# Half of x on a second queue, a first scale made earlier, and a ninth quad of seven products in a one-core hybrid layer

## The chip, the cores and the metric

One core of a Trainium2 chip. The time is device microseconds of one execution; 1537.02 us is the median of three runs of the kernel before (1536.7 to 1537.57). Names of engines: PE is TensorE's matmul, PEld its weight load, DVE is VectorE, ACT is ScalarE, POOL is GpSimd, SP is SyncE, which here issues most of the DMAs.

## The reference

Batch 1, 256 rows, width 2048, one layer, all in fp32:

```python
mod = silu(c) @ ada_w + ada_b            # shift1, scale1, gate1, shift2, scale2, gate2
h = rms_norm(x, norm1_g) * (1 + sc1) + sh1
u, lru_gate, q, k, v, mix_gates = split(h @ w_in + b_in)
y_lru = rg_lru(conv(u)) * gelu(lru_gate)
y_attn = sliding_window_attention(q, k, v, sinks)
g_l, g_a = split(sigmoid(mix_gates))
x = x + g1 * ((g_l * (y_lru @ w_lru_out) + g_a * (y_attn @ w_attn_out)) @ w_o)
h2 = rms_norm(x, norm2_g) * (1 + sc2) + sh2
gate, up = split(h2 @ w_ffn_in)          # hidden width 5632
x = x + g2 * ((silu(gate) * up) @ w_ffn_out)
return rms_norm(x, final_g)
```

## The kernel before

**Products.** Weights are read once, in blocks of 128 x 1024 fp32 (0.5 MB, `raw`). ACT makes a rounded copy of a block (`hi`, L330) and DVE the rest (`lo`, L342), and PE takes three fp32r products for one fp32 product: hi by hi, lo by hi, hi by lo (`mm3`, L382 to L384; L1391 in the last matrix). The work is a list of items, one block each. `step` (L352) goes through it: it first issues what later items need (loads 6 ahead, copies 4, low parts 3), then the item's `before` hooks, then the item's products, then `run_sides`, which puts side work on DVE and ACT (above all the modulation columns) as far as a small model of the engines' clocks (`clock`) finds room. `posts` are what follows an item's last product, one stage of each per step. Every engine works its instructions in order.

**Modulation.** `ada_w` is read transposed, in halves of 0.5 MB (`aw`); one pass of DVE (L532) multiplies a half by the broadcast silu(c) (`crow`) and adds it up to one column of `modc`. 190 passes are needed; the first column of the first scale comes from PE instead (`sum_first`, L213, on two blocks `ak`). A column pair (shift, scale) of kt has to be there before the rows kt of h can be made.

**Opening.** SP issues `vec`, four quarters of x transposed (`xT`, L143), the two `ak` blocks, and then `aw`, `wf` (weights of the first four slabs) and `raw` by turns. PE does warm passes on ones (`keep_warm`, L162; `N_WARM` is how many at three places), broadcasts silu(c) into `crow` (L182), and sums the first scale. ACT squares x quarter by quarter and DVE adds up (`squares`). The sum over partitions (`ssc`) goes to PE between the two halves of `sum_first`; then root, reciprocal, diagonal, a product that spreads the root over partitions (`rx_ps`), and the first `hx`. `First` multiplies k-tiles 0 and 1 in plain fp32 for four slabs (L663), 13.4 us of PE, while `hi`, `lo` and columns for the list are made. The list's first items have few k-tiles each, as `h` comes k-tile by k-tile (`cuts`).

**Second norm.** Items of `w_o` end the first part of the layer; after them `second_norm` follows. `hold_sides`, a hook of the last item but one of `w_o`, stops side work until then. `ada_to(3, 4)`, which makes sure that all columns of shift2 and scale2 are done, is called at the fourth slab of `w_o`.

**Seven products for eight.** From the hidden layer on, some quads (two k-tiles by two column blocks, on two row halves) are done by seven products instead of eight (`seven`, L427). Such a quad needs `wx` (sums of blocks, made by accumulating DMAs that POOL issues 16 and 11 items ahead), `wy` (two DVE additions, L458 and L459) and sums of the left side. A seven has four items, the products of one, two, two and two blocks. In the last matrix (`w_ffn_out`, two halves of 1024 columns, `w_f2a` and `w_f2d`) 18 pairs of k-tiles come in the order of `TURNS`; `SEVEN` says which are sevens. There the left sums are made by `f_parts` in the hidden layer, and split by `parts_high` and `parts_low` (`ah`, `al`, L1404 and L1409), hooks of the two items that stand three and two before a seven's first. After a half's last seven `combined` adds up its banks in five stages, on DVE. The second half ends with eight more items: four for one column block (`w_f2b`) and four, for the upper rows first, of the last block (`w_f2c`), then `last_rows` for the lower rows (`late`), and the final norm.

Of the kernel before, what the change touches and what calls it, by code (L numbers as in the profile page):

```python
# [9 lines left out]
F32 = mybir.dt.float32  # L10
F32R = mybir.dt.float32r
AF = mybir.ActivationFunctionType
# [4 lines left out]
P = 128  # L17
D = 2048
S = 256
# [26 lines left out]

N_K = 1

N_WARM = (6, 15, 5)

N_WARM_2 = (2, 5)

# [12 lines left out]
N_MADE, N_HOLD = 5, 4  # L65

N_SUM = (16, 11)
SEVEN = tuple(range(6, 36, 4))

SEVEN_1, SLAB_7 = (4, 6, 10, 12), 1  # L70

SLAB_G = 4
TURNS_1 = {1: "---7-77-"}

TURNS = "--7-7-7-7-7-7-7-7-"
EARLY = NH - 2 * N_HOLD

N_SPARE = 5
# [5 lines left out]
def hybrid_layer(  # L84
# [21 lines left out]
    def b4(name, dt=F32, shape=(4, S)):  # L106
        used["b4"] += 1
        return bp.tile([P, *shape], dt, tag="b4", name=name)
# [9 lines left out]
    def wtile(name):  # L118
        return ps.tile([P, 2, S], F32, tag="bank", name=name)
# [8 lines left out]
    def rows(t):  # L128
        return slice(t * P, (t + 1) * P)
# [6 lines left out]
    vec = const.tile([P, NV], F32, name="vec")  # L136
    nc.sync.dma_start(vec, vecs)

    def load_x(name):
        ts = []  # L140
        for q in range(4):
            t = b4(f"{name}{q}")
            nc.sync.dma_start(t, x_t[:, 4 * q:4 * q + 4, :])  # L143
            ts.append(t)
        return ts

    xT = load_x("xT")
    first = [b4(f"ak{i}", F32, (NK // 2, P)) for i in range(2)]
    for i in range(2):
        nc.sync.dma_start(first[i], ada_k[i])  # L150
    ones = const.tile([P, P], F32, name="ones")
    nc.vector.memset(ones, 1.0)
    eps_t = const.tile([P, 1], F32, name="eps_t")
# [4 lines left out]
    def keep_warm(n, of_w=False):  # L158

        warm = in_rows_of(wtile("warm")) if of_w else mtile("warm")  # L160
        for _ in range(n):
            nc.tensor.matmul(warm[:, 0:P], lhsT=ones, rhs=ones, start=True, stop=True)  # L162
        free(m=0 if of_w else 1)

    keep_warm(N_WARM[0])

    cact = const.tile([P, NK], F32, name="cact")
# [16 lines left out]

    def squares(q):

        for h in ((slice(0, 4),) if q < 3 else (slice(0, 2), slice(2, 4))):
            nc.scalar.activation(sqx[q][:, h, :], xT[q][:, h, :], AF.Square)
        a = sqx[q]
        for n in (2, 1):  # L190
            nc.vector.tensor_tensor(a[:, 0:n, :], a[:, 0:n, :], a[:, n:2 * n, :], op=ALU.add)
        if q in (1, 2):
            nc.vector.tensor_tensor(a[:, 0, :], a[:, 0, :], sqx[q - 1][:, 0, :], op=ALU.add)

    def c_rows(a, b):
        for i in range(a, b):
            nc.vector.tensor_copy(crow_of(i), c_ps[i])
            free(m=1)

    keep_warm(N_WARM[1])  # L200
    c_rows(0, 1)
    squares(0)
    c_rows(1, 3)
    squares(1)
    c_rows(3, 4)
    squares(2)
    squares(3)

    sc_ps = wtile("sc_ps")[:, 0, 0:P]

    def sum_first(a, b):
        for k in range(a, b):
            nc.tensor.matmul(  # L213
                sc_ps, lhsT=cact[:, k:k + 1].broadcast_to([P, P]), rhs=first[k // 8][:, k % 8, :],
                start=k == 0, stop=k == NK - 1,
            )
# [130 lines left out]
    def upto(what, fn, n):  # L347
        while at[what] < min(n, len(items)):
            fn(at[what])
            at[what] += 1  # L350
# [353 lines left out]
    def ada_to(*ms):  # L704
        while not {(m, kt) for m in ms for kt in range(NK)} <= cols_done:
            if not ada.advance():
                clock["pe"] += 1
                halves.fetch()
# [339 lines left out]
    def load_rows(s):  # L1048
        def before():
            xr.append(b4(f"xr{s}", F32, (2, 512)))  # L1050
            nc.sync.dma_start(xr[s], x_r[:, s * 512:(s + 1) * 512].rearrange("(t p) n -> p t n", p=P))
            if s == 3:
                ada_to(3, 4)
        return before

    def keep_rows(s):
# [29 lines left out]

    def hold_sides():

        clock["slack"] = -1e9
        return 0, 0  # L1090

    items[-2].before.append(hold_sides)

    def turn(p, of_w=False):

# [507 lines left out]
    fetch_to(6)  # L1603
    begin.load(1)

    sum_first(0, NK // 2)
    ssc = mtile("ssc")
    for t in range(2):
        for q in (2, 3):
            nc.tensor.matmul(  # L1610
                ssc[:, t:t + 1], lhsT=sqx[q][:, 0, rows(t)], rhs=ones[:, 0:1], start=q == 2, stop=q == 3,
                skip_group_check=True,
            )
    rc = sp.tile([P, 2], F32, tag="rc", name="rc")
    nc.scalar.activation(rc, ssc[:, 0:2], AF.Sqrt, bias=eps_t, scale=1.0 / D)
    free(m=1)
    sum_first(NK // 2, NK)

    def until(cols):
        while not cols <= cols_done:  # L1620
# [10 lines left out]
    keep_warm(N_WARM[2])  # L1631
    rx = sp.tile([P, S], F32, tag="rx", name="rx", bufs=1)
    nc.scalar.copy(rx, rx_ps)

    dst = modc[:, 1, 0:1]
    nc.vector.tensor_tensor_reduce(
        out=sqx[0][:, 1, 0:P], in0=sc_ps, in1=ident, op0=ALU.mult, op1=ALU.add, scale=1.0,
        scalar=vec[:, V_ADA + NK:V_ADA + NK + 1], accum_out=dst,
    )
    nc.vector.scalar_tensor_tensor(dst, dst, 1.0, vec[:, V_N1:V_N1 + 1], op0=ALU.add, op1=ALU.mult)  # L1640
    cols_done.add((1, 0))
    until({(0, 0)})
    x0 = xT[0][:, 0, :]
    nc.vector.scalar_tensor_tensor(x0, x0, dst, rx_ps, op0=ALU.mult, op1=ALU.mult)
# [16 lines left out]
    upto("hi", do_hi, 1)  # L1661
    upto("lo", do_lo, 1)
    hmod.advance(True)
    for n in range(2):
        begin.post(n)
    upto("hi", do_hi, 2)
    until({(0, 2), (1, 2)})
    fetch_to(14)
    begin.post(2)
    hmod.finish_to(lambda: 2 in h_done)  # L1670
    upto("lo", do_lo, 2)
    upto("hi", do_hi, 3)
    upto("lo", do_lo, 3)
    begin.post(3)
    clock.update(pe=T_START[0], dve=T_START[1], act=T_START[1])
    halves.spare = lambda: len(halves.got) - halves.own < N_SPARE
# [11 lines left out]
def _layout(i):  # L1688
# [10 lines left out]
    def pairs(w):  # L1699
# [13 lines left out]
    w2 = f("w_ffn_out")[0]  # L1713
    a_k = ada_w[:, D:D + P].reshape(2, NK // 2, P, P).transpose(0, 2, 1, 3)
    made = {
        "vecs": vecs, "x_t": f("x")[0].T.reshape(NK, P, S).transpose(1, 0, 2), "x_r": f("x")[0], "ada_k": a_k,
        "ada_t": a_t,
        "w_in": slabs(f("w_in")[0]), "bv_row": f("b_in")[0, 6656:7168], "bm_row": f("b_in")[0, 7168:], "lru_w": lru,
        "w_lru": slabs(f("w_lru_out")[0]), "w_att": slabs(f("w_attn_out")[0]), "w_o": slabs(f("w_o")[0]),
# [25 lines left out]
```

## Time and profile before

| what | us |
|---|---|
| median of three runs | 1537.02 (1536.7 to 1537.57) |
| profiled execution, its own time | 1538.73 |
| its span, first to last instruction | 1537.0 |
| PE busy | 1521.0 |
| DVE busy | 1365.3 |
| ACT busy | 880.7 |

The profile is one execution. Its page gives busy times, strips of 40 slices, the chain of work that ended last, and groups of instructions. Matmuls are pipelined and their ends are modelled, so a row's duration of a product (0.39 us) is longer than the distance to the next (0.228 us); the distances are what PE takes. A wait is put down to the one that came last. The granted clock is given as a share of 2.4 GHz; the other level is 0.50, 1.2 GHz.

### The profile page before, as it was taken

How to read it: one execution, taken by the hardware profiler on the slowest of the kernel's cores; microseconds unless marked ns; L12 is line 12 of the kernel's file. 1: busy time of each engine (PE TensorE's matmuls, PEld its weight loads, DVE VectorE, ACT ScalarE, POOL GpSimd, SP SyncE). 2: the span in 40 equal slices, each digit the busy share in tenths (PEclk: the TensorE clock that was granted, in tenths of full speed). 3: DMA queues.
4: the chain of work that ended last, by engine and by line, in shares of the span. 5: the costliest groups of instructions: out<-in, count | busy, mean ns of one | idle time of the engine just before them, and what ended most of it. 6: DMA issues, size and time to landing. Idle time of an engine off the chain costs nothing.

```text
span 1537.0 us, 20204 instructions
## 1 busy us (share of the span) xinstructions
PE 1521.0 (99%) x6851; PEld 1249.0 (81%) x6851; DVE 1365.3 (89%) x1835; ACT 880.7 (57%) x1142; POOL 163.5 (11%) x232
## 2 busy tenths in 40 slices
PE   8999999999999999999999999999999999999997
PEld 5788888888888787888887878888888888888886
DVE  7999999888898888988988899999999999888987
ACT  4654444886964446444444556656665556664664
POOL 0000000000000000000002231034212122321200
PEclk9999999999999999999999999999999999999999
DMA  9999988656786887999999999589898979989983
GB/s 368 383 345 362 345 315 301 207 181 217 241 286 226 291 308 283 364 325 341 377 373 347 312 338 273 167 254 332 274 273 248 269 243 298 288 257 297 275 266 124
DMA packets 138440, 444.58 MB, mean 289 GB/s; under 512 B 16064, under 2 KB 16224, under 8 KB 138336
## 3 DMA queue, kind: packets, MB, share of 16 engines
q1 hardware_dynamic: 113056, 384.02, 70.2%
q0 software_dynamic: 24992, 58.75, 16.1%
q8 instruction: 53, 0.87, 0.2%
q10 hardware_dynamic: 288, 0.52, 0.1%
q14 instruction: 51, 0.42, 0.1%
HBM read 439.02 MB, written 4.21 MB: 288 GB/s over the span
## 4 chain that ended last, share of the span: by engine, by line
PE 93%; DMA 3%; DVE 3%; ACT 0%; issue 0%; SPq 0%; DVEq 0%; ACTq 0%
PE pf L1391 10%; PE f L383 6%; PE f L382 6%; PE f L384 6%; PE wi L383 6%; PE wi L384 6%; PE wi L382 6%; PE wl L384 2%; PE wl L383 2%; PE wga L384 2%; PE wl L382 2%; PE wga L382 2%; PE wgl L383 2%; PE wga L383 2%; PE wgl L384 2%; PE wa L384 2%
## 5 line engine op out<-in xcount | busy, mean ns | idle before, releaser
L330 ACT CAST hi<-raw 128x1024 fp32r<-128x1024 f32 (+1 forms) x540 | 532.3, 996 | 419.1 <-PE wi L384 87.4
L342 DVE TENSOR_TENSOR lo<-raw,hi 128x1024 fp32r<-128x1024 f32 (+1 forms) x540 | 611.9, 1149 | 82.1 <-issue 37.7
L383 PE MATMUL wi<-lo,h 128*128 128x512 f32 x432 | 168.4, 390 | 3.3 <-DVE lo L342 3.3
L382 PE MATMUL wi<-hi,h 128*128 128x512 f32 x432 | 169.9, 393 | 0.0
L384 PE MATMUL wi<-hi,h 128*128 128x512 f32 x432 | 168.2, 389 | 0.0
L382 PE MATMUL f<-hi,h 128*128 128x512 f32 x406 | 158.8, 391 | 0.0
L383 PE MATMUL f<-lo,h 128*128 128x512 f32 x406 | 158.1, 389 | 0.0
L384 PE MATMUL f<-hi,h 128*128 128x512 f32 x406 | 158.0, 389 | 0.0
L532 DVE CUSTOM_DVE_ANT_0 aw<-aw,crow,vec 128x1024 f32<-128x1024 f32 x95 | 120.5, 1277 | 6.0 <-DMA aw<-in_ada_t_dram 6.0
L532 DVE CUSTOM_DVE_ANT_0 aw<-aw,crow,modc 128x1024 f32<-128x1024 f32 x95 | 121.1, 1277 | 1.6 <-DMA aw<-in_ada_t_dram 1.6
L330 ACT CAST hi<-wy 128x1024 fp32r<-128x1024 f32 x55 | 58.0, 1055 | 74.3 <-PE f L384 32.1
L383 PEld LDWEIGHTS wi<-lo,h 128*128 128x128 f32 x432 | 81.1, 188 | 20.9 <-DVE lo L342 4.3
L342 DVE TENSOR_TENSOR lo<-wx,hi 128x1024 fp32r<-128x1024 f32 x55 | 67.2, 1222 | 32.4 <-issue 28.5
L330 ACT CAST hi<-wx 128x1024 fp32r<-128x1024 f32 x55 | 58.0, 1055 | 64.8 <-PE pf L1391 24.0
L382 PEld LDWEIGHTS wi<-hi,h 128*128 128x128 f32 x432 | 81.1, 188 | 16.8 <-ACT acc L611 0.2
L384 PEld LDWEIGHTS wi<-hi,h 128*128 128x128 f32 x432 | 81.1, 188 | 16.7
L384 PEld LDWEIGHTS f<-hi,h 128*128 128x128 f32 x406 | 76.2, 188 | 15.8
L383 PEld LDWEIGHTS f<-lo,h 128*128 128x128 f32 x406 | 76.2, 188 | 15.7 <-DVE lo L342 0.3
L382 PEld LDWEIGHTS f<-hi,h 128*128 128x128 f32 x406 | 76.2, 188 | 15.6
L447 POOL DMA_DIRECT2D wx<-in_w_f_dram x78 | 69.8, 969 | 79.5 <-DMA wx<-in_w_f_dram 78.4
L443 POOL DMA_DIRECT2D wx<-in_w_f_dram x78 | 44.7, 627 | 287.6 <-DVE lo L342 95.2
L342 DVE TENSOR_TENSOR lo<-wy,hi 128x1024 fp32r<-128x1024 f32 x55 | 67.2, 1222 | 6.9 <-ACT hi L330 4.3
(347 smaller groups left out, 3094.1 us busy)
## 6 DMA issues: line engine op xcount, KB each, us to landing
aw<-in_ada_t_dram SPq DMA_DIRECT2D x190, 512.0 KB, 6.7
raw<-in_w_in_dram SPq DMA_DIRECT2D x164, 512.0 KB, 5.1
raw<-in_w_f_dram SPq DMA_DIRECT2D x137, 512.0 KB, 6.5
wx<-in_w_f_dram POOLq DMA_DIRECT2D x156, 256.0 KB, 7.9
raw<-in_w_f2a_dram SPq DMA_DIRECT2D x36, 512.0 KB, 6.4
raw<-in_w_lru_dram SPq DMA_DIRECT2D x32, 512.0 KB, 4.6
raw<-in_w_att_dram SPq DMA_DIRECT2D x32, 512.0 KB, 5.5
raw<-in_w_o_dram SPq DMA_DIRECT2D x32, 512.0 KB, 8.1
```

The lines of the kernel that those rows point to most:

```text
L330: nc.scalar.copy(hi[:, cs], live[i][0][:, cs])
L342: nc.vector.tensor_tensor(lo[:, cs], raw[:, cs], f32(hi[:, cs]), op=ALU.subtract)
L382: nc.tensor.matmul(ps, lhsT=lh, rhs=rh, start=start, stop=False, skip_group_check=True)
L383: nc.tensor.matmul(ps, lhsT=lh, rhs=rl, start=False, stop=False, skip_group_check=True)
L384: nc.tensor.matmul(ps, lhsT=ll, rhs=rh, start=False, stop=stop, skip_group_check=True)
L443: nc.gpsimd.dma_start(x[:, j * 512:(j + 1) * 512], block(0, 1))
L447: nc.gpsimd.dma_start(got["x"][:, j * 512:(j + 1) * 512], block(j, j), accum_op=ALU.add)
L532: nc.vector.tensor_tensor_reduce(out=r, in0=r, in1=crow[j], op0=ALU.mult, op1=ALU.add, scale=1.0, scalar=dst if j else vec[:, v:v + 1], ac ...
L1391: nc.tensor.matmul(bank(t, n), lhsT=l[:, rows(t)], rhs=w[:, c0:c0 + 512], start=kt == 0 and k == 0, stop=kt == (EARLY - 2 if (t, n) == (1, ...
```

## The change

Opening: x is laid out in four contiguous quarters. SP issues quarters 0 and 2, each before an `ak` block; ACT issues quarters 1 and 3, after a small Silu activation. The 15 warm passes of `N_WARM[1]` (30 records) are gone, the third number goes from 5 to 6. `c_rows` and `squares` are in another order, and the last quarter's squares are added in two halves that go to PE apart. All of `sum_first` and DVE's use of it come before the squares' sums (the diff leaves out the same DVE lines where they stood before, behind `rx`). In the steps before the list, low parts and modulation passes go by turns. At the end of `w_o`, `hold_sides` sits one item earlier and calls `ada_to(3, 4)`. In the last matrix k-tiles 2 and 3 become a seven too: nine of 18, strictly by turns with plain quads.

```diff
-N_WARM = (6, 15, 5)
+N_WARM = (6, 0, 6)
-SEVEN = tuple(range(6, 36, 4))
+SEVEN = tuple(range(2, 36, 4))
-TURNS = "--7-7-7-7-7-7-7-7-"
+TURNS = 9 * "-7"
-    xT = load_x("xT")
+    xT = [b4(f"xT{q}") for q in range(4)]
     first = [b4(f"ak{i}", F32, (NK // 2, P)) for i in range(2)]
-    for i in range(2):
-        nc.sync.dma_start(first[i], ada_k[i])
+    for t, from_ in ((xT[0], x_t[0]), (first[0], ada_k[0]), (xT[2], x_t[2]), (first[1], ada_k[1])):
+        nc.sync.dma_start(t, from_)
...
+    nc.scalar.activation(sp.tile([P, 1], F32, tag="st", name="silu"), eps_t, AF.Silu)
+    for q in (1, 3):
+        nc.scalar.dma_start(xT[q], x_t[q])
     keep_warm(N_WARM[0])
...
-        for h in ((slice(0, 4),) if q < 3 else (slice(0, 2), slice(2, 4))):
-            nc.scalar.activation(sqx[q][:, h, :], xT[q][:, h, :], AF.Square)
         a = sqx[q]
+        if q == 3:
+            for h in range(2):
+                nc.scalar.activation(a[:, 2 * h:2 * h + 2, :], xT[q][:, 2 * h:2 * h + 2, :], AF.Square)
+                nc.vector.tensor_tensor(a[:, 2 * h, :], a[:, 2 * h, :], a[:, 2 * h + 1, :], op=ALU.add)
+            return
+        nc.scalar.activation(a, xT[q], AF.Square)
...
-    keep_warm(N_WARM[1])
-    c_rows(0, 1)
+    sc_ps = wtile("sc_ps")[:, 0, 0:P]
+    c_rows(0, 2)
     squares(0)
-    c_rows(1, 3)
+    c_rows(2, 4)
     squares(1)
-    c_rows(3, 4)
     squares(2)
     squares(3)
...
-            if s == 3:
-                ada_to(3, 4)
...
     def hold_sides():
+        ada_to(3, 4)
         clock["slack"] = -1e9
         return 0, 0
-    items[-2].before.append(hold_sides)
+    items[-3].before.append(hold_sides)
...
-    sum_first(0, NK // 2)
+    sum_first(0, NK)
+    dst = modc[:, 1, 0:1]
+    nc.vector.tensor_tensor_reduce(
+        out=sqx[0][:, 1, 0:P], in0=sc_ps, in1=ident, op0=ALU.mult, op1=ALU.add, scale=1.0,
+        scalar=vec[:, V_ADA + NK:V_ADA + NK + 1], accum_out=dst,
+    )
+    nc.vector.scalar_tensor_tensor(dst, dst, 1.0, vec[:, V_N1:V_N1 + 1], op0=ALU.add, op1=ALU.mult)
+    cols_done.add((1, 0))
     ssc = mtile("ssc")
-    for t in range(2):
-        for q in (2, 3):
+    for i, x in enumerate((sqx[2][:, 0, :], sqx[3][:, 0, :], sqx[3][:, 2, :])):
+        for t in range(2):
...
-    sum_first(NK // 2, NK)
...
     hmod.advance(True)
-    for n in range(2):
-        begin.post(n)
+    begin.post(0)
     upto("hi", do_hi, 2)
+    ada.advance(True)
+    upto("lo", do_lo, 2)
+    begin.post(1)
+    ada.advance(True)
+    ada.advance(True)
+    upto("hi", do_hi, 3)
+    begin.post(2)
+    upto("lo", do_lo, 3)
     until({(0, 2), (1, 2)})
     fetch_to(14)
-    begin.post(2)
     hmod.finish_to(lambda: 2 in h_done)
-    upto("lo", do_lo, 2)
-    upto("hi", do_hi, 3)
-    upto("lo", do_lo, 3)
     begin.post(3)
...
-        "x_t": f("x")[0].T.reshape(NK, P, S).transpose(1, 0, 2)
+        "x_t": f("x")[0].T.reshape(4, 4, P, S).transpose(0, 2, 1, 3)
```

## Rows read from the trace of the kernel before

**Rows 1.** Page, parts 1 and 2: busy us (share) xinstructions; DMA strip, 40 slices

```profile
PE 1521.0 (99%) x6851; PEld 1249.0 (81%) x6851; DVE 1365.3 (89%) x1835; ACT 880.7 (57%) x1142; POOL 163.5 (11%) x232
...
DMA  9999988656786887999999999589898979989983
```

**Rows 2.** Who waited for whom, PE, whole run: us in total, times, longest

```profile
PE wi L383 <- DVE lo L342: 3.3, 2, 1.7
```

**Rows 3.** Chain that ended last, 0 to 62 us: start us, us, what

```profile
1.66 0.42 SPq L143
...
19.88 7.80 DMA raw<-in_w_in_dram
...
39.70 9.22 DMA raw<-in_w_in_dram
...
52.66 0.50 PE wi L383
```

**Rows 4.** Windows: length, busy us of PE, PEld, DVE, ACT, POOL, clock, DMA share, GB/s

```profile
4.00:5.00 1.00, 0.72 (x1) 0.50 (x2) 1.00 (x3) 0.93 (x2) 0.00 (x0) 1.00 0.82 238
```

**Rows 5.** Timeline of ACT in the opening: start us, us, instruction [idle before]

```profile
0.75 1.28 ACT L168 ACT_TABLE_LOAD   x1 [0.75 <-PEq L1733]
...
5.03 1.06 ACT L188 ACTIVATE sqx<-xT 128x1024 f32<-128x1024 f32 x1
8.20 1.06 ACT L188 ACTIVATE sqx<-xT 128x1024 f32<-128x1024 f32 x1 [2.12 <-DMA xT<-in_x_t_dram]
...
10.77 1.15 ACT L188 ACTIVATE sqx<-xT 128x512 f32<-128x512 f32 x2 [0.21 <-DMA xT<-in_x_t_dram]
```

**Rows 6.** Timeline of DVE, 14 to 20 us

```profile
14.75 1.28 DVE L532 CUSTOM_DVE_ANT_0 aw<-aw,crow,vec 128x1024 f32<-128x1024 f32 x1 [0.67 <-DMA aw<-in_ada_t_dram]
...
17.20 0.35 DVE L1636 CUSTOM_DVE_ANT_0 sqx<-sc_ps,ident,vec 128x128 f32<-128x128 f32 x1 [0.77 <-PE sc_ps L213]
...
19.39 0.35 DVE L1646 TENSOR_SCALAR hx<-xT,modc 128x256 f32<-128x256 f32 x1
```

**Rows 7.** Timeline of PE in the opening, warm passes and half of the first scale

```profile
1.06 2.93 PE L162 MATMUL warm<-ones 128*128 128x128 f32 x12 [1.06 <-DVE eps_t L154]
...
9.19 3.51 PE L162 MATMUL warm<-ones 128*128 128x128 f32 x30
...
15.13 2.03 PE L213 MATMUL sc_ps<-ak,cact 128*128 128x128 f32 x16
```

**Rows 8.** Chain, 1296 to 1345 us: plain quads of the last matrix

```profile
1314.86 5.44 PE pf L1391 x24
...
1325.06 5.44 PE pf L1391 x24
```

**Rows 9.** Timeline of DVE at the start of the last matrix

```profile
1301.87 2.95 DVE L342 TENSOR_TENSOR lo<-raw,hi 128x1024 fp32r<-128x1024 f32 x3
1304.75 1.08 DVE L1409 TENSOR_TENSOR al<-fs,ah 128x896 fp32r<-128x896 f32 x1
```

**Rows 10.** Timeline of DVE at the start of its second half

```profile
1411.91 0.69 DVE L1461 TENSOR_TENSOR y<-pf,g 128x512 f32<-128x512 f32 x1 [0.31 <-PE pf L1391]
...
1413.24 1.22 DVE L342 TENSOR_TENSOR lo<-raw,hi 128x1024 fp32r<-128x1024 f32 x1
...
1425.46 1.23 DVE L342 TENSOR_TENSOR lo<-wy,hi 128x1024 fp32r<-128x1024 f32 x1
```

**Rows 11.** DVE at the end: groups of 1500.4 to 1524.1 us, then its timeline

```profile
L342 DVE TENSOR_TENSOR lo<-raw,hi 128x1024 fp32r<-128x1024 f32 x8 | 9.7, 1217 | 0.0
...
1526.67 0.55 DVE L1461 TENSOR_TENSOR y<-late,g 128x384 f32<-128x384 f32 x1
...
1529.11 0.29 DVE L1461 TENSOR_TENSOR y<-late,g 128x128 f32<-128x128 f32 x1 [1.30 <-PE late L384]
```

**Rows 12.** Windows at the second norm, columns as in rows 4

```profile
826.00:829.00 3.00, 1.33 (x9) 0.94 (x8) 2.38 (x6) 2.41 (x7) 0.00 (x0) 1.00 1.09 298
...
830.00:833.00 3.00, 3.00 (x14) 2.81 (x13) 2.55 (x6) 1.62 (x5) 1.98 (x4) 0.50 1.04 406
```

More of the change, by code (lines that the diff above doesn't have):

```diff
@@ L137, in hybrid_layer @@
     nc.sync.dma_start(vec, vecs)
[L139 to L145, printed above, removed]
-    xT = load_x("xT")
+    xT = [b4(f"xT{q}") for q in range(4)]
     first = [b4(f"ak{i}", F32, (NK // 2, P)) for i in range(2)]
-    for i in range(2):
-        nc.sync.dma_start(first[i], ada_k[i])
+    for t, from_ in ((xT[0], x_t[0]), (first[0], ada_k[0]), (xT[2], x_t[2]), (first[1], ada_k[1])):
+        nc.sync.dma_start(t, from_)
     ones = const.tile([P, P], F32, name="ones")
@@ L198, in c_rows @@
             free(m=1)
-    keep_warm(N_WARM[1])
-    c_rows(0, 1)
+    sc_ps = wtile("sc_ps")[:, 0, 0:P]
+    c_rows(0, 2)
     squares(0)
-    c_rows(1, 3)
+    c_rows(2, 4)
     squares(1)
-    c_rows(3, 4)
     squares(2)
     squares(3)
-    sc_ps = wtile("sc_ps")[:, 0, 0:P]
     def sum_first(a, b):
@@ L1604, in hybrid_layer @@
     begin.load(1)
-    sum_first(0, NK // 2)
+    sum_first(0, NK)
[6 more added lines that the diff above has]
+    cols_done.add((1, 0))
     ssc = mtile("ssc")
-    for t in range(2):
-        for q in (2, 3):
+    for i, x in enumerate((sqx[2][:, 0, :], sqx[3][:, 0, :], sqx[3][:, 2, :])):
+        for t in range(2):
             nc.tensor.matmul(
-                ssc[:, t:t + 1], lhsT=sqx[q][:, 0, rows(t)], rhs=ones[:, 0:1], start=q == 2, stop=q == 3,
+                ssc[:, t:t + 1], lhsT=x[:, rows(t)], rhs=ones[:, 0:1], start=i + t == 0, stop=i == 2,
                 skip_group_check=True,
@@ L1633, in hybrid_layer @@
     nc.scalar.copy(rx, rx_ps)
[L1635 to L1641, printed above, removed]
     until({(0, 0)})
@@ L1715, in _layout @@
     made = {
-        "vecs": vecs, "x_t": f("x")[0].T.reshape(NK, P, S).transpose(1, 0, 2), "x_r": f("x")[0], "ada_k": a_k,
+        "vecs": vecs, "x_t": f("x")[0].T.reshape(4, 4, P, S).transpose(0, 2, 1, 3), "x_r": f("x")[0], "ada_k": a_k,
         "ada_t": a_t,
```

## The prediction

> **What bounds the kernel now.** I read part 1 and the strips of the page first, then who waited for whom on PE, then the chain, then the timelines of the three places the diff touches. PE is busy 99% of the span, so a change has to take products away or close one of PE's few gaps [rows 1]. Over the run PE waits 3.3 us, in two waits, for a low part in the input projection, and nothing else costs it as much [rows 2]. The strip of the DMA engines is full in its first slices [rows 1]: the opening lives on transfers. The chain shows it. A weight block issued at 19.88 needs 7.80 us to land, one issued at 39.70 needs 9.22 us, and the second of PE's waits ends at 52.66, 3.7 us after that block landed at 48.92 [rows 3]. So PE's state at 52.7 us is set by how many bytes have come, not by when PE began. From there to the two waits at the second norm PE has no wait over 0.2 us, so whatever the opening gains or loses by 52.7 is carried to the end.
>
> **Opening, transfers.** Four quarters of x (2.1 MB) and two blocks of the first scale (1.05 MB) come ahead of the modulation columns and weights. The same bytes come before and after; two of the quarters now go out on ACT's queue and interleave with SP's. Only an emptier stretch of the DMA engines can give time back. Between 4 and 5 us they moved 238 GB/s [rows 4]. ACT's square of the second quarter waited 2.12 us for it, until 8.20; the next two quarters were there by 10.77 [rows 5], 1.28 us each (0.52 MB, 408 GB/s). The second came 3.2 us after the first (5.0), so at most 1.9 us are to be had. From the other side, ACT issues its first quarter only behind a table load that ends at 2.03 and an added 0.2 us activation, 0.6 us later than SP issued it (1.66) [rows 3, 5]: 0.6 us can be lost. I take a gain of 0.5 us, nearer to no change, because the first quarter, in the same layout, showed no such lag, and the later blocks all run at the full rate: it looks like a matter of the first microseconds rather than of the layout or the queue. The Trainium skill (DMA: Bandwidth & Descriptors, "Issuing engines are not separate DMA queues") says that starting transfers from several engines saves only the issuing time, as all run on the same 16 engines. By that rule the gain is nothing and the sum 0.5 us longer; the issue of 0.42 us for a quarter that takes 1.28 us bears it out so far.
>
> **Opening, order.** The first scale's 32 passes now all run before the squares' sums, and DVE's work on them (0.35 and 0.16 us) stands ahead of its first modulation pass. Before, that pass ran at 14.75 and DVE then stood until 17.20 for the scale [rows 6]. That looks like 1.2 us. But the second scale block is still the last of the same 3.3 MB and lands near 13.3; its 16 passes take 2.03 us [rows 7], so DVE gets the scale at 15.3, and the pass that ran at 14.75 now waits behind it until 15.9. The two passes, the root's reciprocal and diagonal (0.5 us) and the two steps of `hx` then end at about 19.6 against 19.74 now [rows 6]: nothing won. Low parts by turns with passes closes the first wait (1.7 us at 36.8 to 38.3): the second item's low part no longer stands behind four passes. It is not banked: the fourth item's low part still comes after the same DVE work, at 42.4, and the eighth item waits for its block at 48.9 as before. PE's idle 1.7 us there is the cover that hides all of this. The 30 warm passes (3.51 us) taken out and one fp32 pass added (0.25 us) lie in PE's waiting.
>
> **Second norm.** `hold_sides` comes one item earlier; the columns it demands are done by 742 us, so `ada_to` does nothing in either place. One modulation pass (1.28 us) moves from before the norm to after it. The low part that gates the norm is bound by its own block's landing, so I take 0, between -0.3 and +0.5. Slab 0 of the hidden layer now makes a sum form of one pair: 0.3 us more on DVE, beside PE.
>
> **Ninth quad.** A plain quad is 24 products in 5.44 us, and plain and seven together recur every 10.20 us, so a seven takes 4.76 [rows 8]. One more in each half: 2 x 0.68 = 1.36 us less PE. In the steady alternation DVE has 1.4 us free in 10.2, and nothing changes there. The edges change, since a quad of plain products that stood as a cushion at the start and end of each half is gone.
> Start of the first half: DVE finishes the hidden layer's last gating at 1301.87 [rows 9]. Before, two plain quads (10.9 us) follow; now one, and DVE must do a half low part (0.6), `al` (1.0), `wy` (1.33) and a low part (1.22) by the seven's second item: 1306.0. PE reaches that product at 1303.6 + 0.8 (transposes) + 0.68 + 0.23 = 1305.3: 0.7 us of stall, 0 to 1.2.
> Start of the second half: four residual pairs of 1.33 us (1411.91 to 1413.24) interleave with the same list. From 1413.2: 0.6, 1.0, 1.33, 1.33, 1.13, 1.33, 1.13, 1.33, 1.22 end the `wy` low part at 1423.6; before it ended at 1426.7 [rows 10]. PE wants it at 1413.3 + 5.44 + 0.68 + 2 x 1.36 + 0.23 = 1422.4: 1.2 us, 0 to 1.6.
> The end: after the last product of sevens (1500.3) DVE works without a break until it takes the first late block at 1526.67, and the second at 1529.11, when PE has it; eight subtractions cost 9.7 us there [rows 11]. Now PE has one plain quad less to run after that product (5.44), DVE two subtractions less (2.3). DVE reaches the second late block at 26.4 - 2.3 + 1.1 = 25.2 us after it, or 24.9 if its small waits go too, and PE at 28.8 - 5.44 = 23.4. The last rows become DVE's: 1.5 us, 0 to 2.
>
> **Sum.** -0.5 (opening) + 0 (norm) - 1.36 + 0.7 + 1.2 + 1.5 = +1.5, which I round down to +1.4 because small DVE waits can close. The profiled execution took 1538.73 us (span 1537.0, 1.7 around it), so it would take 1540.1; the median of the runs lies 1.7 lower, and 1537.02 becomes **1538.4 us**. With the bounds of the terms it goes from about 1536 to 1541.
>
> **Rivals.** *DVE keeps up.* Its queue has three low parts in hand at each edge; if the orders mesh, no stall shows. For it: the page has hardly any such wait now. Against: the counts above. -1.36 - 0.5: 1535.2.
> *Both gains arrive.* The quarters come at the late rate (1.9 us) and the edges are covered: -3.3, 1533.7, faster. For it: the slow stretch is exactly the second quarter.
> *The clock falls in the opening,* the slower one. PE loses its 30 passes and stands idle from 9.4 until the first scale block is here. At the second norm, after a stretch with 1.33 us of products in 3, the granted clock went from 1.00 to 0.50 [rows 12], that is from 2.4 to 1.2 GHz. The first 12 warm passes took 2.93 us, the later 30 took 3.51 [rows 7], so at the low level 32 passes cost 4 us more, and the first products begin near 23.5 and run 3 us or more at half speed. The cover of 1.7 us is then used up and about 2 us remain: 1540.6. It decides if the first block lands after about 11 us, and not if it lands at 10, as I expect from its place behind two quarters. The Trainium skill (TensorE: Matmul & The Clock Gate, "Why this matters for your kernels") warns against idle gaps between bursts for this reason; that gap in this kernel is not yet in any row.
>
> **How the numbers follow.** Forecast (DVE takes the quads' gain back) 0.55, DVE keeps up 0.20, both gains 0.13, clock 0.12. 0.2% is 3.1 us, about what runs of this kernel can tell from no change: faster means under 1533.9, slower over 1540.1. Faster: the third case and a little of the second, 0.15. Slower: most of the clock's case and the top of the forecast's, 0.15. Same: 0.70. The range takes in the forecast with its bounds and both outer cases: 1533.5 to 1541.0.
>
> **What would show it.** Right: PE's wait near 38 us gone, the one near 50 us still there and ended by DVE behind a landed block; PE waits for DVE of about a microsecond soon after the first plain quad of each half; DVE idle-free to the last two late blocks, with PE done first. Wrong: first weight blocks landing over 1.5 us earlier than 27.7; no wait at the halves' starts; a clock of 0.50 between 10 and 25 us.

## The result, and the profile after

The changed kernel takes 1542.86 us (median of five runs, 1541.19 to 1544.38) beside 1536.7 for the kernel before (five runs, 1536.09 to 1537.57): 1.0038 times as long, 95% interval 1.0024 to 1.0051. It is slower; 1538.4 was forecast. The profiled execution of after took 1542.86 with a span of 1541.1.

PE has less work, as the change means it to, and DVE more. The page's part 1 answers [rows 1].

```profile
PE 1518.0 (99%) x6821; PEld 1244.1 (81%) x6821; DVE 1373.6 (89%) x1848; ACT 885.1 (57%) x1150; POOL 169.0 (11%) x240
```

PE's waits of the whole run answer [rows 2]: us in total, times, longest.

```profile
PE wi L381 <- DVE lo L340: 3.2, 2, 1.7
PE fr L381 <- DVE lo L340: 1.4, 1, 1.4
...
PE pu L380 <- DVE fl L989: 0.9, 1, 0.9
...
PE pq L381 <- DVE lo L340: 0.8, 1, 0.8
...
PE pf L381 <- DVE lo L340: 0.5, 1, 0.5
PE f L381 <- DVE lo L340: 0.4, 1, 0.4
```

The two waits of the opening are still there (`wi`, one now for the fourth item's low part, until 42.2, the other until 52.3). New are two in the hidden layer's second slab (`f`, `fr`, at 902 to 905 us) and three at the starts of the last matrix's halves (`pf`, `pu`, `pq`). Windows show the first pair's price: length, busy us of the engines, granted clock, DMA share, GB/s.

```profile
826.00:829.00 3.00, 2.16 (x17) 1.92 (x16) 1.50 (x6) 1.17 (x5) 0.00 (x0) 1.00 1.07 326
830.00:833.00 3.00, 3.00 (x17) 2.48 (x17) 2.81 (x8) 1.38 (x4) 0.61 (x2) 1.00 0.98 395
...
902.00:906.00 4.00, 2.22 (x8) 1.26 (x7) 4.00 (x6) 2.51 (x3) 1.98 (x3) 0.94 1.12 227
905.00:909.00 4.00, 3.52 (x9) 2.80 (x9) 3.96 (x6) 1.09 (x2) 1.06 (x2) 0.57 1.08 301
```

At the second norm the clock now stays at 1.00, where [rows 12] have 0.50. Behind the two waits at 902 to 905 it falls instead to 0.50, 1.2 GHz: nine products in four us where, at 0.228 us each, seventeen fit.

DVE's timeline at the starts of the two halves answers [rows 9] and [rows 10]; the last two lines are the end, as in [rows 11].

```profile
1302.18 0.69 DVE L340 TENSOR_TENSOR lo<-raw,hi 128x512 fp32r<-128x512 f32 x1
1302.78 1.08 DVE L1406 TENSOR_TENSOR al<-fs,ah 128x896 fp32r<-128x896 f32 x1
...
1305.12 1.22 DVE L340 TENSOR_TENSOR lo<-raw,hi 128x1024 fp32r<-128x1024 f32 x1
1306.25 1.22 DVE L340 TENSOR_TENSOR lo<-wx,hi 128x1024 fp32r<-128x1024 f32 x1
1307.39 1.22 DVE L340 TENSOR_TENSOR lo<-wy,hi 128x1024 fp32r<-128x1024 f32 x1
1308.52 1.28 DVE L989 TENSOR_TENSOR fl<-ft,fh 128x512 fp32r<-128x512 f32 x2
...
1413.45 0.69 DVE L1458 TENSOR_TENSOR y<-pf,g 128x512 f32<-128x512 f32 x1
...
1423.98 1.22 DVE L340 TENSOR_TENSOR lo<-wy,hi 128x1024 fp32r<-128x1024 f32 x1
...
1531.91 0.55 DVE L1458 TENSOR_TENSOR y<-late,g 128x384 f32<-128x384 f32 x1
...
1532.97 0.28 DVE L1458 TENSOR_TENSOR y<-late,g 128x128 f32<-128x128 f32 x1
```

The list at 1302 to 1308 is the one counted in the prediction, with `fl` behind it, which was not counted. At the end DVE takes both late blocks (`late`) without a pause between them, and PE's last product is over at 1531.4: the end waits for DVE, as forecast.

Distances between products give what each place costs. The stretch from the first product behind the second norm to `g_ps` (the next gate) took 178.8 us before and 181.2 after. The last matrix, from its first product to its last, took 230.9 and 232.9: 1.36 us less work, 1.85 us of waits at the first half's start and 1.44 at the second's. From PE's last product to the end of the span there are 7.9 and 9.6 us. These three lengths are followed through the experiments.

### The profile page after: what moved, and what is told of

It reads as the page before. It is cut to its first block, busy times and chain, and to the rows that moved or that the text cites. A ratio compares the mean times of both kernels' runs of the same rounds, so it can differ in the third digit from the quotient of the medians.

```text
span 1541.1 us, 20198 instructions
## 1 busy us (share of the span) xinstructions
PE 1518.0 (99%) x6821; PEld 1244.1 (81%) x6821; DVE 1373.6 (89%) x1848; ACT 885.1 (57%) x1150; POOL 169.0 (11%) x240
## 5 line engine op out<-in xcount | busy, mean ns | idle before, releaser
L1388 PE MATMUL pf<-hi,fc 128*128 128x512 f32 x288 | 79.9, 389 | 0.0
L445 POOL DMA_DIRECT2D wx<-in_w_f_dram x78 | 69.8, 979 | 83.8 <-DMA wx<-in_w_f_dram 83.1
```

The costliest lines, as they stand in the source:

```text
L445: nc.gpsimd.dma_start(got["x"][:, j * 512:(j + 1) * 512], block(j, j), accum_op=ALU.add)
L1388: nc.tensor.matmul(bank(t, n), lhsT=l[:, rows(t)], rhs=w[:, c0:c0 + 512], start=kt == 0 and k == 0, stop=kt == (EARLY - 2 if (t, n) == (1, ...
```

## Experiments

Times are medians; the ratio is to the kernel before on the same chip (medians of 1535.7 to 1536.7 by group), with its 95% interval. It is not simply the quotient of the two medians, and can differ from it by up to 0.001. The last three columns are the lengths just named, from the one profiled execution of each run.

| run | us | ratio | hidden | last matrix | end |
|---|---|---|---|---|---|
| before | 1536.7 | | 178.8 | 230.9 | 7.9 |
| after | 1542.86 | 1.0038 [1.0024, 1.0051] | 181.2 | 232.9 | 9.6 |
| hold_alone | 1538.54 | 1.0019 [1.0010, 1.0028] | 180.2 | 230.9 | 7.9 |
| quads_alone | 1540.54 | 1.0029 [1.0019, 1.0040] | 178.7 | 232.9 | 9.6 |
| opening_alone | 1536.93 | 0.9998 [0.9989, 1.0007] | 177.9 | 230.9 | 8.1 |
| quads_back | 1539.82 | 1.0021 [1.0012, 1.0030] | 182.8 | 230.9 | 8.1 |
| hold_back | 1540.71 | 1.0030 [1.0019, 1.0041] | 178.2 | 233.0 | 9.9 |
| pair_12 | 1543.40 | 1.0052 [1.0039, 1.0064] | 180.4 | 233.0 | 9.8 |
| no_load | 1539.74 | 1.0022 [1.0012, 1.0032] | 178.2 | 233.0 | 9.9 |
| no_pass | 1540.77 | 1.0029 [1.0019, 1.0039] | 179.9 | 233.0 | 9.6 |
| cushion | 1539.14 | 1.0020 [1.0009, 1.0031] | 178.7 | 234.2 | 8.2 |
| no_wy | 1538.40 | 1.0014 [1.0005, 1.0023] | 178.2 | 230.3 | 9.9 |
| fl_early | 1540.08 | 1.0024 [1.0014, 1.0034] | 180.3 | 232.6 | 9.9 |
| pool_wy | 1544.78 | 1.0059 [1.0047, 1.0072] | 179.7 | 239.0 | 10.1 |
| opening_warm | 1535.64 | 0.9995 [0.9986, 1.0004] | 178.8 | 230.9 | 8.1 |
| opening_sp | 1536.83 | 1.0003 [0.9993, 1.0013] | 179.9 | 230.9 | 8.1 |

### Which part costs

**quads_back** is the changed kernel with the sevens as they were:

```diff
-SEVEN = tuple(range(2, 36, 4))
+SEVEN = tuple(range(6, 36, 4))
-TURNS = 9 * "-7"
+TURNS = "--7-7-7-7-7-7-7-7-"
```

> The changed kernel with its eight sevens per half and their old order back; opening, second norm and hold_sides stay as changed. The two traces, laid side by side, give this ledger against the kernel before: opening -0.3, second norm -3.0 (1.7 of it a stretch at clock 0.50 that is gone), a stall with a stretch at clock 0.50 behind it at 902 to 909 us +3.2, starts of the halves +3.3, the products saved -1.4, the end +1.8. Theory S (slab 0's sum form, which only the ninth seven needs, makes DVE late at 902 us): stall and edges go, the norm's gain stays, 1533 to 1534.5. Theory P (the modulation pass moved behind the norm makes it late): the stall stays, 1536.5 to 1537.5, and PE waits over 1 us for a low part near 903 us. In both the halves' starts have no wait over 0.3 us.

The waits near 903 stay (`f` 1.8, `fr` 1.4 us), so slab 0's sum form, theory S, is out. The last matrix and its end are back to 230.9 and 8.1. But the time, 1539.82, is 2 to 3 us over what theory P gave. The ledger in that expectation had booked 3 us of gain at the norm as the change's, read from one profile against one. From the last product of `w_o` to the first behind the norm all other runs take 5.3 to 6.6 us, with `hold_sides` in either place; only that execution of before took 8.4. About 1.1 of this is its low clock (ten warm passes took 2.34 us there and 1.28 in after); ahead of it PE had already waited 1.0 us for `xr`.

**quads_alone** is the kernel before with the two lines of the diff above the other way round.

> The kernel before with nothing changed but the ninth seven and the strict alternation in the last matrix. Edge theory: +3.3 at the starts of the halves, -1.4 for the products, +1.8 at the end, 3.7 us over the kernel before, 1540.4. With theory S (slab 0's sum form) the stall at 902 to 909 us comes on top: 1543 to 1544. With theory P there is no such stall, 1540 to 1541. If the rival that DVE keeps up were right after all and the other parts of the change were to blame: 1535.3.

1540.54, the edge theory's number, with no long wait near 903. The ninth seven alone costs 1.0029.

**hold_back** is the changed kernel with one line changed back:

```diff
-    items[-3].before.append(hold_sides)
+    items[-2].before.append(hold_sides)
```

> The changed kernel with hold_sides put back on the last item but one, so that one modulation pass more runs ahead of the second norm. Theory P: the norm's gain of 3.0 goes and with it the stall at 902 us and its low clock (3.2): 1542.5 to 1543. Theory S: the norm's gain goes and the stall stays: 1545 to 1546. A third way: the norm's gain did not come from hold_sides but from what ran before it; then norm and stall stay as in the changed kernel, 1542.9, and the products after the norm begin near 829.4 as there, not near 831.9.

The waits near 903 go (one of 0.4 us is left) and nothing is lost at the norm: about 2 us less than the numbers of theory P and of the third way, and 4 to 5 less than theory S's, for the reason just given.

**hold_alone** is the kernel before with that line the other way round, and `ada_to(3, 4)` moved with it.

> The kernel before with nothing changed but hold_sides one item earlier (and ada_to with it). In the traces the stretch from the first product behind the second norm to g_ps takes 177.9 to 178.8 us where hold_sides is in its old place and 180.4 to 182.8 where it is in its new one, and the norm itself (last product of w_o to first behind the norm, without the one execution that had a stretch at clock 0.50 there) 5.3 to 6.6 in both. Theory D (a third modulation load in front of two weight blocks): two to four us lost, 1538 to 1540, with a wait of over 1 us near 903 to 906. Rival: only the new opening brings PE early enough to meet the late blocks; here it does not wait, 1535.7 to 1536.5.

```profile
PE fr L383 <- DVE lo L342: 1.5, 2, 1.4
PE f L383 <- DVE lo L342: 0.4, 1, 0.4
```

These are its waits between 885 and 915 us, the same as in after without the new opening or the new quads, and it costs 1.0019.

**opening_alone** joins the edits of quads_back and hold_back, so that only the opening is changed.

> The changed kernel with hold_sides back on the last item but one and the eight sevens per half in their old order: only the opening is changed. In the traces of the four kernels with this opening the last product of w_o ends at 822.8 to 823.2, in the two with the old one at 823.4 and 823.7. Theory: that half microsecond is all the opening gives, 1535.5 to 1536.0, with no stall near 903 and the end of the last matrix as before. Rival: stretches at clock 0.50 between 10 and 45 us, which three of those four show and one of the two old ones, cost what the transfers give: 1536.2 to 1537.5.

0.9998: no difference that can be measured, though the median is 1.2 us above that of the kernel before in its group (1535.7). One of its two stretches at 0.50 lies at 53 us, behind the last wait of the opening, and this execution ends `w_o` at 825.0; the other ten with this opening (of after and the runs here, without opening_warm and opening_sp) end it at 822.7 to 823.5, the three with the old one at 823.4 to 824.3. The gain of half a microsecond is there and is as large as the scatter.

The ratios of hold_alone, quads_alone and opening_alone add up to 1.0046; after has 1.0038, within the intervals.

### What holds PE near 903 us

**pair_12** takes k-tiles 12 and 13 for 2 and 3, so that slab 0 has no sum form.

```diff
-SEVEN = tuple(range(2, 36, 4))
+SEVEN = tuple(sorted((*range(6, 36, 4), 12)))
```

> The changed kernel with nine sevens per half in the same order, but k-tiles 12 and 13 in place of 2 and 3, so that slab 0 needs no sum form and slab 3 needs two. Theory S: the stall at 902 to 909 us goes, 1539 to 1540, and the products at 915 us stand 3 us earlier than in the changed kernel. Theory P: the stall stays, 1542.5 to 1543. Edges at the halves' starts and the end as in the changed kernel in both.

Theory P: 1543.40, 0.4 us above its range, and the waits stay (`fr` 1.6, `f` 0.7).

So it is the modulation work that no longer runs ahead of the norm. A modulation half is a load of 0.5 MB on SP and a pass on DVE. Behind the first product after the norm DVE makes eleven passes in after and ten in hold_back; SP issues seven loads there in both, but in another order. SP's queue of after, then of hold_back, at the place where the weight blocks of 892 to 898 us are issued:

```profile
876.88 0.33 SPq L311 DMA_DIRECT2D raw<-in_w_f_dram  x1
877.26 1.77 SPq L501 DMA_DIRECT2D aw<-in_ada_t_dram  x3
879.12 0.38 SPq L311 DMA_DIRECT2D raw<-in_w_f_dram  x1
```

```profile
874.49 0.33 SPq L311 DMA_DIRECT2D raw<-in_w_f_dram  x1
874.87 0.90 SPq L501 DMA_DIRECT2D aw<-in_ada_t_dram  x2
876.44 3.05 SPq L311 DMA_DIRECT2D raw<-in_w_f_dram  x2
```

In after three `aw` stand between two weight blocks, in hold_back two; the next block lands 9.3 us after the one ahead of it in after (883.0 to 892.3) and 7.5 in hold_back (882.7 to 890.2). Behind that block DVE's queue has one pass more, ahead of the low part of `wx` that `fr` needs. DVE in after, from that block on, then in hold_back:

```profile
899.86 1.28 DVE L530 CUSTOM_DVE_ANT_0 aw<-aw,crow,modc 128x1024 f32<-128x1024 f32 x1
...
903.01 1.28 DVE L530 CUSTOM_DVE_ANT_0 aw<-aw,crow,modc 128x1024 f32<-128x1024 f32 x1
...
904.21 1.22 DVE L340 TENSOR_TENSOR lo<-wx,hi 128x1024 fp32r<-128x1024 f32 x1
```

```profile
897.78 1.28 DVE L530 CUSTOM_DVE_ANT_0 aw<-aw,crow,modc 128x1024 f32<-128x1024 f32 x1
...
900.92 1.22 DVE L340 TENSOR_TENSOR lo<-wx,hi 128x1024 fp32r<-128x1024 f32 x1
```

Two kernels part load and pass. Both leave one column of the second gate wrong.

```diff
-                nc.sync.dma_start(t, self.srcs[self.n])
+                if self.n == 189:
+                    nc.gpsimd.memset(t, 0.0)
+                else:
+                    nc.sync.dma_start(t, self.srcs[self.n])
```

> The changed kernel, but the last of the modulation's 190 halves is not loaded: its tile is filled with zeros by POOL, so one column of the second gate is wrong. In the changed kernel three such loads go out in a row on SP at 877.3 to 878.7, ahead of two weight blocks that land at 892.3 and 894.9; in the kernel before and with hold_sides put back there are two. Theory D (the transfer stands ahead of the weight blocks): those blocks land 1.3 us earlier or more, the waits of 0.4 and 1.4 us for low parts near 903 go, and what follows stands 2 to 3.4 us earlier, 1539.5 to 1541. Theory V (DVE's pass stands ahead of the low part): the blocks land earlier, and the wait of 1.2 to 1.4 us near 904 stays, 1542 to 1543.

```diff
+    n_passes = []
...
+                    n_passes.append(kt)
+                    if len(n_passes) != 190:
                         nc.vector.tensor_tensor_reduce(
...
```

> The changed kernel, but the last of the 190 modulation passes is left out on DVE (1.28 us), while its half is still loaded, so one column of the second gate is wrong. Theory V: the low part of the block sum follows without it, the wait near 904 is at most 0.3 us and what follows stands 2 to 3.4 us earlier, 1539.5 to 1541. Theory D: the blocks land as late as in the changed kernel, the high and low parts with them, and a wait of over 1 us stays near 903, 1542 to 1543.

PE's waits between 885 and 915 us in no_load, then ACT's copies of the blocks there, with their idle time:

```profile
PE fr L381 <- DVE lo L340: 0.4, 2, 0.2
```

```profile
891.61 1.99 ACT L328 CAST hi<-raw 128x1024 fp32r<-128x1024 f32 x2
894.86 1.05 ACT L328 CAST hi<-raw 128x1024 fp32r<-128x1024 f32 x1 [1.26 <-PE f L382]
```

The same two views of no_pass:

```profile
PE f L381 <- DVE lo L340: 1.1, 1, 1.1
PE fr L381 <- DVE lo L340: 0.4, 2, 0.2
```

```profile
892.90 1.05 ACT L328 CAST hi<-raw 128x1024 fp32r<-128x1024 f32 x1 [0.86 <-DMA raw<-in_w_f_dram]
895.50 1.05 ACT L328 CAST hi<-raw 128x1024 fp32r<-128x1024 f32 x1 [1.55 <-DMA raw<-in_w_f_dram]
```

Without the load ACT no longer waits for these blocks, and both long waits go although DVE still makes the pass, as theory D has it. Without the pass ACT waits for the blocks as before and one wait of 1.1 us stays, as in theory D; but the wait at `fr` goes, as in theory V, and the time, 1540.77, lies in theory V's range and not in theory D's. The times of the two runs do not decide: their intervals overlap. Nor does no_load prove that the loads' order is to blame, since one load less would let the block land earlier with `hold_sides` in either place.

A comparison over all runs helps: when does the weight block behind the last `aw` land, counted from the first product behind the norm? In the ten runs with the old place of `hold_sides` and all their modulation work it lands at 61.1 to 64.6 us, and the hidden length follows it: 177.9 to 178.2 where it lands by 62.0, 178.7 and 178.8 at 62.5 to 62.9, 179.7 at 63.9 (pool_wy), 179.9 at 64.1 (opening_sp), 180.3 at 64.6 (fl_early). In the four with the new place it lands at 63.0 to 64.8. Their hidden lengths of 180.2 to 182.8 are longer than an equally late landing gives with the old place, by 0.5 to 1.3 us once 1.7 us are taken off for the stretch at 0.50 that two of them, after and quads_back, have behind these waits. no_pass, at 64.0 and 179.9, lies with the old place. So the pass is what the new place adds at an equal landing, and only where the block lands late: no_load, with the pass, loses nothing at 61.1 (178.2). Whether the new order of loads also makes the block land later (63.5 us in the mean of these four, 62.9 in the mean of the ten) is not shown: the ten scatter by more than that.

### The ends of the halves

**cushion** is hold_back with two plain quads at each half's start and one at its end:

```diff
-TURNS = 9 * "-7"
+TURNS = "--7-7-7-77-7-77-7-"
```

> The same opening and the old place of hold_sides, with nine sevens per half, but two plain quads at the start of each half and one at its end as in the kernel before; three plain quads fewer stand between sevens, so two pairs of sevens follow each other without a plain one. Edge theory: no wait at the halves' starts, PE's end and the tail as with eight sevens, and the products saved stay saved: 1.4 us less than opening_alone, 1534 to 1534.6. Rival, DVE theory: DVE's work per seven, not the edge, is what is missing; a double seven then costs a wait of 0.7 us or more for a low part, four of them 3 us: 1537 or more.

Both theories had a part. No wait is left at the starts, and the end is back to 8.2 us. But each of the four places where two sevens follow each other costs 1.1 us:

```profile
PE pf L381 <- DVE lo L340: 3.4, 4, 0.9
```

The last matrix is the longest but one, 234.2 us. A plain quad between two sevens is itself the cushion; neither order tried leaves DVE the time for a ninth seven.

**no_wy** takes hold_back and leaves two DVE additions out at each half's first seven:

```diff
+            if by_k and begin:
+                return got["x"], 1.3
             y = bp.tile([P, CH], F32, tag="b4", name="wy")
```

> The changed kernel with hold_sides put back, in which the first seven of each half of the last matrix takes the block sum wx a second time in place of wy, so that two DVE additions (1.33 us) go and its products are not the reference's. DVE theory of the halves' starts: in the changed kernel the first half's start costs 1.85 us more than full pace and the second's 1.44; without the additions DVE is 1.33 us earlier, and 0.5 and 0.1 to 0.4 are left, 2 to 2.5 us less than with hold_sides put back alone (1540.7): 1538.2 to 1538.8; the end stays, 9.7 us from PE's last product to the end of the span. Rival: the waits hang on transfers of the raw blocks or on ACT; then they stay and the time is 1540.5 to 1541.

The starts fall from 3.3 us to 0.7, one wait at `pu`, by twice 1.33 as DVE's work does. The end stays at 9.9.

**fl_early** (hold_back again) issues the two subtractions `fl` of slab 10 together with their copy, which puts them ahead of one low part:

```diff
-        yield 0, 1.2
+        if not now:
+            yield 0, 1.2
...
-            yield from parts_of(pts, fh, fl)
+            yield from parts_of(pts, fh, fl, s == 10)
```

> The changed kernel with hold_sides put back, and in the hidden layer's last slab the two subtractions that read the transposes (fl) one stage earlier, ahead of the low part of wy instead of behind it. Bank theory (pu's bank is the one that fl frees): the wait of 1.0 us ahead of the first product into pu falls to 0.3 or less, and one for the low part of wy, now 1.2 us later, of 0.3 to 0.7 comes in its place a product later: 0.3 to 0.6 us less than with hold_sides put back alone (1540.7). Rival, DVE is late there by its sum of work: the wait at pu stays at about 1 us, time within 0.3 of 1540.7.

PE's waits in the last matrix, of hold_back, then of fl_early:

```profile
PE pu L380 <- DVE fl L989: 0.8, 1, 0.8
PE pq L381 <- DVE lo L340: 0.8, 1, 0.8
PE pf L381 <- DVE lo L340: 0.5, 1, 0.5
```

```profile
PE pq L381 <- DVE lo L340: 1.2, 2, 0.8
PE pf L381 <- DVE lo L340: 0.5, 1, 0.5
```

The wait at `pu` is gone, and one of 0.4 to 0.6 us for the low part that now runs later has come: the bank theory, with a net of 0.3 us in the last matrix. This execution also waited 1.2 us near 892 and 0.5 near 903 (hidden 180.3). Its edit, 400 us later, does not explain that; the late landing, at 64.6, does. As the hidden stretch scatters so, the price of `hold_sides` rests on hold_alone's interval more than on one row.

**pool_wy** (hold_back) lets POOL make `wy` in the last matrix:

```diff
-            nc.vector.tensor_tensor(y[:, 0:512], got["x"][:, 0:512], raw(1, 1), op=ALU.add)
-            nc.vector.tensor_tensor(y[:, 512:], y[:, 0:512], raw(1, 0), op=ALU.add)
+            eng = nc.gpsimd if by_k else nc.vector
+            eng.tensor_tensor(y[:, 0:512], got["x"][:, 0:512], raw(1, 1), op=ALU.add)
+            eng.tensor_tensor(y[:, 512:], y[:, 0:512], raw(1, 0), op=ALU.add)
```

> The changed kernel with hold_sides put back, in which POOL instead of DVE makes wy for all sevens of the last matrix (18 times two additions, 1.33 us each time on DVE). If POOL keeps up: no wait over 0.5 us at the halves' starts, DVE early enough for the late blocks, so that the end is near 8 us again; -3.3 -1.8 against 1540.7: 1535.5, and faster than the kernel before by up to 1 us if the saved products (1.4) stay. Rival: an addition takes POOL so long, or holds up its own accumulating transfers or DVE so much, that PE waits for wy in every seven: 1545 or more.

The rival's side, though PE does not wait in every seven. Apart from the wait at the first half's start, it waits at four sevens of the second half alone, for two reasons. At 1422.8 it waits 2.4 us, and at 1496.8 another 0.7, for low parts that POOL's additions held up on DVE (rows in the last section). At 1477, 1499 and 1500 it waits 3.2 us in all for ACT's copy and DVE's low part of `wy`, which themselves stood behind POOL's slow additions: ACT waited 3.8 and 5.5 us for them. A stretch at 0.50 behind the first of these waits (1424.2) adds 1.7 us to this execution, which took 2.1 us more than the median.

### The opening

**opening_warm** adds to opening_alone 12 warm passes ahead of `c_rows`:

```diff
-N_WARM = (6, 0, 6)
+N_WARM = (6, 6, 6)
+    keep_warm(N_WARM[1])
     c_rows(0, 2)
```

> The kernel with the changed opening alone, and 12 of the 30 warm passes back between the broadcasts and the first scale (1.2 us of PE, in its wait for the first scale's blocks). In eight executions with the new opening seven had a stretch at clock 0.50 between 10 and 54 us, four of them near 42, three near 16; of two with the old opening one had. Theory: the stretch near 16 comes from PE's idle stretch from 8 to 14 and goes; the one near 42 comes behind the wait for the fourth item's low part and stays. As both lie ahead of the wait near 50 that a landing ends, the time is that of the opening alone, 1535.7 to 1536.9. Rival: the low clock costs there what the transfers gave, and without it the time is 1535 to 1535.5.

The stretch near 16 us is absent and one at 42.5 is there. 1535.64, 0.9995: the smallest time of all, but not to be told from the kernel before, nor from opening_alone.

**opening_sp** issues all of x on SP, ahead of the first scale's two blocks (edits against opening_alone):

```diff
-    for t, from_ in ((xT[0], x_t[0]), (first[0], ada_k[0]), (xT[2], x_t[2]), (first[1], ada_k[1])):
+    for t, from_ in (*zip(xT, x_t), (first[0], ada_k[0]), (first[1], ada_k[1])):
...
-    for q in (1, 3):
-        nc.scalar.dma_start(xT[q], x_t[q])
```

> The changed opening alone (hold_sides and sevens as in the kernel before), but all four quarters of x go out on SP in order, ahead of the two blocks of the first scale; x keeps its new layout. Queue theory: between 4 and 6 us the transfers fall back to 238 to 262 GB/s and the first high-part block comes 0.3 us later in its first pieces (25.9 instead of 25.5). Layout theory: they stay at 400 to 418 GB/s, and the first pieces at 25.4 to 25.6. By either the time is within 0.5 us of the opening alone (1536.9, ratio 0.9998 to the kernel before), as the wait near 50 us hides most of it.

Windows of after, then of opening_sp:

```profile
4.00:5.00 1.00, 0.61 (x2) 0.31 (x3) 1.00 (x3) 0.99 (x2) 0.00 (x0) 1.00 1.02 414
5.00:6.00 1.00, 1.00 (x4) 0.55 (x3) 1.00 (x2) 0.05 (x1) 0.00 (x0) 1.00 1.03 410
```

```profile
4.00:5.00 1.00, 0.78 (x2) 0.47 (x3) 1.00 (x3) 0.87 (x2) 0.00 (x0) 1.00 1.07 418
5.00:6.00 1.00, 1.00 (x3) 0.39 (x3) 1.00 (x3) 0.87 (x1) 0.00 (x0) 1.00 0.99 295
8.00:10.00 2.00, 0.00 (x0) 0.00 (x0) 2.00 (x4) 1.06 (x1) 0.00 (x0) 1.00 1.01 410
10.00:12.00 2.00, 0.59 (x3) 0.62 (x4) 1.90 (x5) 1.15 (x2) 0.00 (x0) 0.69 1.05 408
```

On SP alone the rate is 418 GB/s from 4 to 5 us, and 295 from 5 to 6: the layout and the queue each have a part, and neither theory holds alone. The three kernels with the old opening moved 238 to 287 GB/s from 4 to 5 us and 262 to 336 from 5 to 6. The last of the six blocks (x and first scale) landed at 13.3 in before, 12.5 in opening_sp and 11.4 in after. The first block of the first scale, which now stands behind all of x, lands at 11.3 instead of 9.1. PE stands idle from 7.9 to 11.4, the clock falls at 10.8, and the first product comes at 23.8 instead of 18.0. `w_o` ends at 824.1, one microsecond later than in the others, and the time is that of the kernel before.

## Why the prediction was wrong, by its steps

1538.4 was forecast and 1542.86 measured, 4.5 us more. The steps that failed carry 2.4 to 2.9 (second norm: hold_alone, and quads_back less opening_alone), 1.4 (starts of the halves) and 0.2 (the end); the opening's 0.5 did not show in the time.

**Second norm: the step that failed most.** "One modulation pass (1.28 us) moves from before the norm to after it" was priced at the norm, at 0 with +0.5 as its bound. At the norm that held (5.3 to 6.6 us in both places). What was left out is where the work comes to stand behind it: some 70 us on, between a weight block that lands late and the low part of `wx` that PE wants, DVE makes two passes where it made one, and ahead of that block SP issues three `aw` in a row and not two. hold_alone measured +2.4 us (1.0019, 1.0010 to 1.0028) for the whole; how much of it is the pass and how much the order of the loads stays open. A moved side job has to be followed to its new place, on the DMA queue as well as on DVE. The sum form of slab 0, counted as hidden beside PE, did stay hidden (pair_12).

**Ninth quad, products.** -1.36 us forecast; 230.9 - 1.36 + 3.3 of waits is 232.8, and 232.9 was measured.

**Start of the first half.** 0.7 forecast; the low part that it was worked out for costs 0.75, at the product named (run at 1306.4). The other 1.1 us is the product into `pu`, whose bank the hidden layer's transposes still hold until `fl`. Before, two plain quads hid `fl` too. The list of DVE's work stopped one entry early (fl_early).

**Start of the second half.** 1.2 forecast, 1.44 measured: 0.35 for the low part of `wx`, 1.1 for that of `wy`, which ended at 1425.2 instead of 1423.6. The first was not forecast.

**The end.** 1.5 forecast, 1.7 measured, by the mechanism described: DVE is last. That DVE works "without a break" up to the late blocks was misread: before and after it waits 0.85 and 0.36 us for ACT there. So the quads cost 3.7 us in the trace where the terms gave 2.0; quads_alone's 1.0029 [1.0019, 1.0040], 2.9 to 6.1 us, agrees.

**Opening, transfers.** -0.5 forecast; -0.6 between the medians of `w_o`'s end (823.05 and 823.7), 0.9998 in time: right in size by luck, and too small to be measured. Its reasons were wrong. The layout and the queue do have a part (opening_sp), against the rule that the prediction quoted for the queue, and the first scale's blocks came 1.9 us earlier, the bound named for both gains. The 0.6 us that ACT's late issue might lose were not lost: ACT issues its two quarters at 1.07, while its table load runs until 2.02 and the activation follows at 2.04.

```profile
1.07 0.90 ACTq L160 DMA_DIRECT2D xT<-in_x_t_dram  x2
```

But 0.3 us was left of the 1.9 at 28.7: the weight block issued at 19.4 landed there, against 29.0 before, and the block of the wait near 50 landed at 48.6 against 48.9. From the last block of the first scale to that one the same bytes took 35.6 to 36.6 us in the three kernels with the old opening and 36.9 to 37.6 in the twelve with two queues. So most of the gain was lost again in the transfers, not hidden by PE's wait; why they lag is not shown.

**Opening, order.** `hx` "at about 19.6" was wrong: 18.0, since the second block came at 11.4 and not 13.3. It brought nothing to the time, for the reason given there: the wait near 50 is set by a landing, and took up what PE gained. The wait near 38 moved to the fourth item's low part at 42.2, for which 42.4 was forecast.

**Rivals.** DVE keeps up, and both gains arrive: refuted by the waits. *The clock falls in the opening:* more was in it than its chance of 0.12. Of eleven executions with this opening nine had a stretch at 0.50 between 15 and 45 us, four near 16 and five near 42. Its own condition is met in opening_sp (block at 11.3, first products at 23.8 where it said 23.5). But its price was too high: 1 us at the end of `w_o` and not 2, and nothing where the stretch came near 16 or 42 with no other behind the last wait. The Trainium skill (TensorE: Matmul & The Clock Gate, "Why this matters for your kernels") has an idle gap between bursts drop the clock. opening_sp agrees: PE was idle from 7.9 to 11.4 us, and the clock fell at 10.8. The falls near 16, 42 and 905 us came behind shorter ones, waits of 1.2 to 1.7 us.

The chances failed with the sum: every case kept `hold_sides` at 0, and the bound of each edge was drawn around one counted list.

## What to carry to other kernels

Work that is moved past a stall goes somewhere: follow each of its instructions, its loads too, to the place where it now queues, and look what stands behind it there. Where a cushion of spare work is taken away at an edge, list everything that the slower engine has in its queue there, with reads that free a bank, and not only the chain to the first wait. An earlier start that ends at a wait for a landing buys nothing. One profile against one can book a chance stretch of low clock, or a late landing, as a gain or a loss: compare several, at an equal landing.

## What the runs showed of the hardware

**POOL's additions hold DVE up.** The same place in pool_wy, POOL's two additions and DVE's instructions beside them:

```profile
1418.26 1.68 POOL L457 TENSOR_TENSOR wy<-wx,raw 128x512 f32<-128x512 f32 x1
1418.70 0.68 DVE L1459 TENSOR_TENSOR y<-pf,g 128x512 f32<-128x512 f32 x1
1419.42 1.07 DVE L1461 TENSOR_TENSOR x<-y,x 128x512 f32<-128x512 f32 x1
1420.02 1.60 POOL L458 TENSOR_TENSOR wy<-wy,raw 128x512 f32<-128x512 f32 x1
1420.41 2.29 DVE L340 TENSOR_TENSOR lo<-wy,hi 128x1024 fp32r<-128x1024 f32 x1
```

An addition takes POOL 1.6 and 1.7 us here (1.9 to 2.0 in the mean of 18), against 0.69 on DVE. The low part, 1.22 us elsewhere, took 2.29 and ended 1.1 us behind POOL; an addition of two SBUF tiles took 1.07 instead of 0.69. The product with a PSUM operand (`y<-pf,g`) took its usual 0.68 in the middle of POOL's addition. The Trainium skill (SBUF — State Buffer, "SBUF: two separate sides") says that POOL and DVE instructions with two SBUF inputs exclude each other for a whole instruction; these rows agree. Elsewhere in this run DVE's low parts took up to 3.05 us, and POOL's additions up to 5.0.

**The same program meets the low clock at different places.** Behind one and the same wait for the fourth item's low part the clock fell in six executions and stayed at 1.00 in others; at the second norm it fell in one execution of all. A low stretch there is a matter of the execution, and what it cost depended on its cover: near 42 nothing that shows at the end of `w_o`, behind the waits near 903 about 1.7 us in after and quads_back, while hold_alone and pair_12 had the same waits at a clock of 1.00.
